# Weight sums moved from GpSimd to VectorE, and low parts of weights made by accumulating DMAs, in the pooling layer of a two-layer encoder trunk

## The chip, the cores and the metric

One core of a Trainium2 chip runs the whole program. The metric is the device time of one execution in microseconds (us). TensorE is called PE in the profile, VectorE DVE, ScalarE ACT, GpSimd POOL and SyncE SP; SP issues the plain loads.

## The reference

A sequence of 512 tokens of width 1024 passes two residual layers. The even layer (mLSTM heads and stick-breaking attention heads) is not touched by the change. The odd layer is:

```python
def odd_layer(x, pre_g, post_g, w_in, pool_w, pool_scale, w_out):
    h = rmsnorm(x, pre_g)
    u = h @ w_in                                  # 512x1024 @ 1024x4096
    p, z = u[..., :C_WIDTH], u[..., C_WIDTH:]     # 2048 columns each
    pooled = multiscale_pool(p.reshape(Bn, S, C_GROUPS, C_GROUP_DIM))   # windows 2, 4, 8, 16
    mixed = jnp.einsum('bsgc,gce->bsge', pooled, pool_w)                # 4 maps of 512x512
    mixed = mixed.reshape(Bn, S, C_WIDTH) * pool_scale
    y = (mixed * jax.nn.silu(z)) @ w_out                                # 512x2048 @ 2048x1024
    return x + rmsnorm(y, post_g)
```

`multiscale_pool` is the mean over a trailing window of each channel, one window for each group of 512 channels, minus the token itself. Everything is float32.

## The kernel before, in words

**Precision.** TensorE multiplies float32r, a rounded float32. Each operand x is kept as a high part, x rounded to float32r, and a low part, x minus the high part. A product is three matmuls (`mm3`, lines 95 to 97): high by high, high by low, low by high. `split` makes both parts: ACT copies with rounding into the high tile (line 71), then DVE subtracts it from x into the low tile (line 72). `halves` does that for weights, into the tiles `wh` and `wl`, of which four slots each go round in the order in which the program asks for them. A new weight block can be split only when TensorE has made the last use of the block four places earlier.

**Loads.** `load` brings 1024 KB of raw weights into one of two `w32` tiles, issued by SP (line 83).

**The odd layer** goes over four groups g = 0 to 3, with windows 2, 4, 8 and 16. Each group has two blocks p (columns to be pooled) and two blocks z (gates), named pg0, pg1, zg0, zg1, each 1024 by 256 weights against 512 tokens. Group 0's p comes from plain projections; the other 14 blocks go through `strassen2`, a seven-product scheme. It cuts a block of raw weights into a11, a12, a21, a22 (each 128 x 512 in a tile), and builds four sums on GpSimd (lines 695 to 698): s1 = a21 + a22, s2 = s1 + a11, s3 = a11 + a21, s4 = a12 + s2. Then it splits four weight tiles:

- a: the raw left half, a11 and a21 (128 x 1024), for the first two products,
- b: the sums s2 and s1 (128 x 1024),
- c: the sums s3 and s4 (128 x 1024),
- d: a22 (128 x 512), for the last product.

Each product is 12 matmuls of 256 columns. Products go into the banks psa, psb and pse, and DVE and ACT combine them (lines 715 to 732; the `pt` tiles hold partial results). The right-hand operands are blocks of the layer's input `hTh`/`hTl` and four combinations of them (d3, d1, n2, t4), which DVE forms once in `hidden_sums`.

**Pooling** of a group's four chunks of 128 channels: DVE adds shifted copies (line 762) and finishes with line 769; POOL divides the first few columns (lines 767, 768) and clears edges with memsets; `split` makes `pph` and `ppl`. The group's 512 x 512 map `pw` is split in two halves and multiplied with them in 48 matmuls of 512 columns into `mx`.

**Order.** The program is written in tiles, and a scheduler lays out each engine's instructions in one fixed order at build time. Each engine then works strictly in that order, waiting on semaphores. So a change of one operation reorders whole engines in the layer.

Of the kernel before, what the change touches and what calls it, by code (L numbers as in the profile page):

```python
# [5 lines left out]
F32 = mybir.dt.float32  # L6
F32R = mybir.dt.float32r
AF = mybir.ActivationFunctionType
ALU = mybir.AluOpType
# [4 lines left out]
P = 128  # L14
S = 512
# [21 lines left out]
def body(nc, tc, x, pre_g, post_g, w_in, conv, b_i, b_f, hn_g, w_out, w_in_c, pool_w,  # L37
         pool_scale, w_out_c, out):
    V, A, G, T = nc.vector, nc.scalar, nc.gpsimd, nc.tensor
# [4 lines left out]
    with base as base, psum as psum, dram as dram:  # L44
# [4 lines left out]
        def pj(name): return bank("pj", 2, name)  # L49
# [20 lines left out]
        def split(src, hi, lo):  # L70
            A.activation(hi, src, AF.Copy)  # L71
            V.tensor_tensor(lo, src, hi.bitcast(F32), op=ALU.subtract)  # L72

        def whl(name):
            return (base.tile([P, WIDE], F32R, tag="wh", bufs=4, name=f"wh_{name}"),
                    base.tile([P, WIDE], F32R, tag="wl", bufs=4, name=f"wl_{name}"))
# [9 lines left out]
        def halves(w, name, into=None):  # L86

            a, n = w.shape[1], w.shape[2]
            wh, wl = (t[:, :a * n].rearrange("p (a n) -> p a n", a=a) for t in (into or whl(name)))
            split(w, wh, wl)  # L90
            return wh, wl
# [110 lines left out]
        with tc.tile_pool(name="att", bufs=1) as at:  # L202
# [386 lines left out]
            for h in range(HA):  # L589
# [7 lines left out]
                for s in range(NB):  # L597
                    t = bc[:, ROW[s]:ROW[s] + P]
# [28 lines left out]
        with tc.tile_pool(name="odd", bufs=1) as od:  # L627
# [6 lines left out]
            def big(name, dtype=F32): return od.tile([P, D], dtype, tag="big", bufs=8, name=name)  # L634

            def ytiles(n):
                return (od.tile([P, S], F32R, tag="phi", bufs=5, name=f"yh_{n}"),
                        od.tile([P, S], F32R, tag="plo", bufs=5, name=f"yl_{n}"))

            ready = y_split(1, EVEN2[0], ytiles("first"), "e")  # L640
            xn = od.tile([P, NB, D], F32, name="xn")
# [28 lines left out]
            def ws(name): return od.tile([P, 8, P], F32, tag="ws", bufs=3, name=name)  # L670

            def hidden_sums():
                raw = {}
                b11, b21, b12, b22 = quarter(0, 0), quarter(1, 0), quarter(0, 1), quarter(1, 1)
                for n in ("d3", "d1", "n2", "t4"):
# [9 lines left out]
                        V.scalar_tensor_tensor(raw[n], raw["n2"], -1.0, b21, op0=ALU.mult, op1=ALU.subtract)  # L685
                    split(raw[n], *hs[n])

            def strassen2(src, name, dsts, silu=False):

                w = load(lambda t: [(nc.sync, t, src)], 8, 256, name)  # L690
                a11, a12, a21, a22 = (w[:, 4 * k:4 * k + 4, m * P:m * P + P]
                                      for m in range(2) for k in range(2))
                sums = [ws(f"ws{i}_{name}") for i in range(2)]
                s1, s2, s3, s4 = sums[0][:, 4:], sums[0][:, :4], sums[1][:, :4], sums[1][:, 4:]
                G.tensor_tensor(s1, a21, a22, op=ALU.add)  # L695
                G.tensor_tensor(s2, s1, a11, op=ALU.add)
                G.tensor_tensor(s3, a11, a21, op=ALU.add)
                G.tensor_tensor(s4, a12, s2, op=ALU.add)
                first = halves(w[:, :, :P], f"{name}_a")
                second = halves(sums[0], f"{name}_b")  # L700
                third = halves(sums[1], f"{name}_c")
                fourth = halves(a22, f"{name}_d")

                def product(ps, wt, k0, b, start, stop):
                    (wh, wl), (bh, bl) = wt, hs[b]
                    for k in range(4):
                        mm3(ps, (wh[:, k0 + k], wl[:, k0 + k]), (bh[:, k], bl[:, k]),
                            start and k == 0, stop and k == 3, skip_group_check=True)

                def part(i): return od.tile([P, 256], F32, tag="part", bufs=4, name=f"pt{i}_{name}")  # L710

                pa, pb, pe = (f(f"ps{n}_{name}")[:, :256] for f, n in ((pj, "a"), (xa, "b"), (xb, "e")))
                t1, t2, t5 = part(1), part(2), part(5)
                product(pa, first, 0, "11", True, True)
                A.activation(t1, pa, AF.Copy)
                product(pb, first, 4, "21", True, True)
                V.tensor_tensor(dsts[0][:, :256], pb, t1, op=ALU.add)
                product(pa, second, 0, "n2", False, True)
                A.activation(t2, pa, AF.Copy)
                product(pe, second, 4, "d1", True, True)  # L720
                A.activation(t5, pe, AF.Copy)
                product(pa, third, 0, "d3", False, True)
                V.scalar_tensor_tensor(dsts[1][:, 256:], pa, -1.0, t5, op0=ALU.mult, op1=ALU.subtract)
                product(pe, third, 4, "22", False, True)
                V.tensor_tensor(dsts[0][:, 256:], pe, t2, op=ALU.add)
                product(pa, fourth, 0, "t4", False, True)
                if silu:
                    act(dsts[0], dsts[0], AF.Silu)
                    act(dsts[1][:, 256:], dsts[1][:, 256:], AF.Silu)
                    act(dsts[1][:, :256], pa, AF.Silu, scale=-1.0)  # L730
                else:
                    A.activation(dsts[1][:, :256], pa, AF.Copy, scale=-1.0)

            for g, w in enumerate(WINDOWS):
                pooled = []
                cur4 = []
                for j in range(4):
                    c = 4 * g + j
                    cur = od.tile([P, 16 + S], F32, tag="win", bufs=6, name=f"p_{c}")
                    G.memset(cur[:, :16], 0.0)  # L740
                    cur4.append(cur)
                wsrc = [w_in_c[0, :, 512 * g + 256 * i:512 * g + 256 * i + 256] for i in range(2)]
                if g == 0:
                    wj = [t() for i in range(2) for t in col_load(wsrc[i], f"p{g}{i}")]
                    for j, n0 in ((j, n0) for n0 in (0, 256) for j in range(4)):
                        ps = pj(f"ps_p{4 * g + j}_{n0}")
                        col_proj(wj[j], ps, n0, n0 + 256)
                        A.activation(cur4[j][:, 16 + n0:16 + n0 + 256], ps[:, n0:n0 + 256], AF.Copy)
                    hidden_sums()
                else:  # L750
                    for i in range(2):
                        strassen2(wsrc[i], f"p{g}{i}", [t[:, 16:] for t in cur4[2 * i:2 * i + 2]])
                for j in range(4):
                    c = 4 * g + j
                    cur = cur4[j]
                    p32 = cur[:, 16:]
                    sh = 1
                    while sh < w:
                        nx = od.tile([P, 16 + S], F32, tag="win", bufs=6, name=f"p_{c}_{sh}")
                        if 2 * sh < w:  # L760
                            G.memset(nx[:, :16], 0.0)
                        V.tensor_tensor(nx[:, 16:], cur[:, 16:], cur[:, 16 - sh:16 + S - sh],  # L762
                                        op=ALU.add)
                        cur, sh = nx, 2 * sh
                    sm = cur[:, 16:]
                    e = w - 1
                    G.tensor_tensor(sm[:, :e], sm[:, :e], invc[:, :e], op=ALU.mult)
                    G.tensor_tensor(sm[:, :e], sm[:, :e], p32[:, :e], op=ALU.subtract)
                    V.scalar_tensor_tensor(sm[:, e:], sm[:, e:], 1.0 / w, p32[:, e:], op0=ALU.mult,
                                           op1=ALU.subtract)  # L770
                    ph = od.tile([P, S], F32R, tag="phi", bufs=5, name=f"pph{c}")
                    pl = od.tile([P, S], F32R, tag="plo", bufs=5, name=f"ppl{c}")
                    split(sm, ph, pl)
                    pooled.append((ph, pl))
                sz = []
                for i in range(2):
                    pair = [od.tile([P, S], F32, tag="sz", bufs=4, name=f"sz{4 * g + 2 * i + j}")
                            for j in range(2)]
                    strassen2(w_in_c[0, :, 2048 + 512 * g + 256 * i:2304 + 512 * g + 256 * i],
                              f"z{g}{i}", pair, True)  # L780
                    sz.extend(pair)
                w4 = load(lambda t: [(nc.sync, t, pool_w[0, g])], 4, 512, f"pw{g}")
                pw = [halves(w4[:, 2 * i:2 * i + 2], f"pw{g}{i}") for i in range(2)]
                for e in range(4):
                    c = 4 * g + e
                    ps = ac(f"mx{c}")
                    for k in range(4):
                        wh, wl = pw[k // 2]
                        mm3(ps, (wh[:, k % 2, e * P:e * P + P], wl[:, k % 2, e * P:e * P + P]),
                            pooled[k], k == 0, k == 3)  # L790
                    V.scalar_tensor_tensor(y32[:, c], ps, psc(c), sz[e], op0=ALU.mult, op1=ALU.mult)
# [44 lines left out]
```

## Time and profile before

| | us |
|---|---|
| median of 3 runs | 935.57 (935.47 to 936.04) |
| profiled execution | 938.04 |
| its span in the trace | 936.3 |
| odd layer's groups, in the span | about 605 to 845 |
| output map behind them | about 845 to 929 |

The profile counts the busy time of each engine in the span. In its timeline, idle time ahead of an instruction stands in square brackets with the instruction that ended it. The granted TensorE clock is given as a share of full speed for a stretch of time. Names in the trace leave out group numbers: `wl_z_a` is the low part of a of any z block.

### The profile page before, as it was taken

The numbers are of one execution on the slowest core, as the hardware profiler recorded it, in microseconds if no ns is written. First come the engines' busy times: TensorE is split into PE (matmuls) and PEld (weight loads), VectorE is DVE, ScalarE is ACT, GpSimd is POOL, SyncE is SP. The second block draws the span as 40 slices with busy tenths as digits, with TensorE's granted clock in tenths as the row PEclk, the third lists the DMA queues.
The fourth block names the chain that finished last, engine by engine and source line by source line (L and its number), as shares of the span: only waits on it lengthen the run. The fifth ranks groups of instructions, "written<-read, shape, count | busy, mean of one in ns | idle before, by whom it ended". The sixth has DMA issues, their size and how long they took to land. (4 is left out here: it accounts for less than half of the span.)

```text
span 936.3 us, 12756 instructions
## 1 busy us (share of the span) xinstructions
PE 903.9 (97%) x4957; PEld 783.1 (84%) x4957; DVE 603.9 (65%) x863; ACT 503.3 (54%) x850; POOL 170.4 (18%) x277
## 2 busy tenths in 40 slices
PE   8999999999999999999999999988989999889997
PEld 6788889888988898898888878888979988868885
DVE  5435555658876673854855556677695887957452
ACT  6436666665776554555467455654434544535331
POOL 2001111101102001010010000065565456510000
PEclk8999999999999999999999999998989999989998
DMA  8232221212222233223312645503122241346331
GB/s 293 89 93 66 71 90 46 90 48 88 80 97 90 85 93 127 91 91 124 96 45 90 225 174 196 169 1 130 51 91 90 91 136 46 114 134 223 109 117 46
DMA packets 67133, 98.97 MB, mean 106 GB/s; under 512 B 2848, under 2 KB 54136, under 8 KB 67072
## 3 DMA queue, kind: packets, MB, share of 16 engines
q1 hardware_dynamic: 65888, 98.08, 32.1%
q8 instruction: 39, 0.64, 0.3%
q10 hardware_dynamic: 1184, 0.08, 0.1%
q14 instruction: 22, 0.18, 0.1%
HBM read 96.02 MB, written 2.13 MB: 105 GB/s over the span
## 5 line engine op out<-in xcount | busy, mean ns | idle before, releaser
L97 PE MATMUL ps_qa<-hTh,wl_qa 128*128 128x512 f32 x128 | 50.3, 393 | 0.0
L95 PE MATMUL ps_qa<-hTh,wh_qa 128*128 128x512 f32 x128 | 50.2, 393 | 0.0
L96 PE MATMUL ps_qa<-hTl,wh_qa 128*128 128x512 f32 x128 | 50.2, 392 | 0.0
L72 DVE TENSOR_TENSOR wl_wo_e<-w_wo_e,wh_wo_e 128x1024 fp32r<-128x1024 f32 x28 | 34.3, 1233 | 23.5 <-ACT wh_wo_e L71 23.3
L71 ACT ACTIVATE wh_wo_e<-w_wo_e 128x1024 fp32r<-128x1024 f32 x28 | 29.4, 1057 | 29.0 <-DMA w_wo_e<-in_w_out_ab 13.6
L540 PE MATMUL op<-wh_wo_e,yl_e 128*128 128x512 f32 x120 | 39.1, 396 | 0.0
L540 PE MATMUL op<-wl_wo_e,yh_e 128*128 128x512 f32 x120 | 39.1, 396 | 0.0
L762 DVE TENSOR_TENSOR p<-p 128x512 f32<-128x512 f32 x40 | 37.9, 955 | 0.1
L540 PE MATMUL op<-wh_wo_e,yh_e 128*128 128x512 f32 x120 | 37.8, 395 | 0.0
L384 POOL TENSOR_TENSOR w<-w,w 128x384 f32<-128x384 f32 (+2 forms) x12 | 10.4, 869 | 144.8 <-DVE pl L72 135.9
L67 ACT ACT_TABLE_LOAD x28 | 35.9, 1283 | 1.3 <-PEq L821 0.8
L97 PE MATMUL psv_va<-wh_va,hTl 128*128 128x256 f32 x128 | 36.1, 282 | 0.0
L95 PE MATMUL psv_va<-wh_va,hTh 128*128 128x256 f32 x128 | 36.1, 282 | 0.0
L96 PE MATMUL psv_va<-wl_va,hTh 128*128 128x256 f32 x128 | 36.1, 282 | 0.0
L695 POOL TENSOR_TENSOR ws_z<-w_z 128x512 f32<-128x512 f32 x8 | 17.8, 2229 | 98.6 <-DVE d1l L72 69.0
L320 DVE SCALAR_TENSOR_TENSOR cv<-u,vecs,cv 128x511 f32<-128x511 f32 (+2 forms) x48 | 35.4, 748 | 0.4
L447 POOL TENSOR_SCALAR_AFFINE_SELECT a<-a 128x128 f32<-128x128 f32 x32 | 12.1, 387 | 126.9 <-DVE a L445 111.3
L72 DVE TENSOR_TENSOR wl_wo_o<-w_wo_o,wh_wo_o 128x1024 fp32r<-128x1024 f32 x20 | 24.3, 1224 | 12.0 <-ACT wh_wo_o L71 12.0
L72 DVE TENSOR_TENSOR wl_qa<-w_qa,wh_qa 128x1024 fp32r<-128x1024 f32 x16 | 19.6, 1222 | 18.4 <-ACT wh_qa L71 18.4
L540 PE MATMUL oq<-wl_wo_o,yh_o 128*128 128x512 f32 x96 | 31.3, 405 | 0.0
L540 PE MATMUL oq<-wh_wo_o,yh_o 128*128 128x512 f32 x96 | 31.3, 404 | 0.0
L71 ACT ACTIVATE wh_wo_o<-w_wo_o 128x1024 fp32r<-128x1024 f32 x20 | 20.9, 1053 | 19.2 <-PE oq L540 8.1
(430 smaller groups left out, 3210.1 us busy)
## 6 DMA issues: line engine op xcount, KB each, us to landing
w_wo_e<-in_w_out_ab SPq DMA_DIRECT2D x14, 1024.0 KB, 4.8
w_wo_o<-in_w_out_c SPq DMA_DIRECT2D x12, 1024.0 KB, 5.0
w_qa<-in_w_in_ab SPq DMA_DIRECT2D x8, 1024.0 KB, 5.0
w_p<-in_w_in_c SPq DMA_DIRECT2D x8, 1024.0 KB, 5.4
w_z<-in_w_in_c SPq DMA_DIRECT2D x8, 1024.0 KB, 5.3
w_qb<-in_w_in_ab SPq DMA_DIRECT2D x4, 1024.0 KB
w_kb<-in_w_in_ab SPq DMA_DIRECT2D x4, 1024.0 KB, 5.0
w_zb<-in_w_in_ab SPq DMA_DIRECT2D x4, 1024.0 KB, 5.0
```

Of the source, the lines that this page charges most:

```text
L67: link(A.preload_act_table_set(TABLE[func]))
L71: A.activation(hi, src, AF.Copy)
L72: V.tensor_tensor(lo, src, hi.bitcast(F32), op=ALU.subtract)
L95: T.matmul(dst, lhsT=ah, rhs=bh, start=first, stop=False, **kw)
L96: T.matmul(dst, lhsT=ah, rhs=bl, start=False, stop=False, **kw)
L97: T.matmul(dst, lhsT=al, rhs=bh, start=False, stop=last, **kw)
L320: V.scalar_tensor_tensor(acc[:, j:], u[:, :S - j], cw(3 - j, c), acc[:, j:], op0=ALU.mult, op1=ALU.add)
L384: G.tensor_tensor(total[:, t0:], total[:, t0:], w[:, t0:], op=ALU.add)
L447: G.affine_select(a[:, t0:t0 + P], a[:, t0:t0 + P], pattern=[[1, P]], base=-1, channel_multiplier=-1, compare_op=ALU.is_ge, fill=0.0)
L540: T.matmul(ps[a][n], lhsT=l[:, ta], rhs=r[:, 0, n * 512:n * 512 + 512], start=(first and l is yh and r is wh), stop=(last and l is yl))
L695: G.tensor_tensor(s1, a21, a22, op=ALU.add)
L762: V.tensor_tensor(nx[:, 16:], cur[:, 16:], cur[:, 16 - sh:16 + S - sh], op=ALU.add)
```

## The change

The four sums go from GpSimd to VectorE. For the raw weights, a and d, and for both halves of each pool map, a new function makes the low part without VectorE: ACT writes the rounded weights negated into the low tile, GpSimd issues DMAs that add the raw weights from memory onto it, and ACT writes the high tile as before. What lands is raw minus rounded, the same low part. A DMA covers 128 x 4 x 128 numbers (256 KB, in rows of 512 B) for a strassen block, two for a and one for d; and 128 x 2 x 512 (512 KB, in rows of 2 KB) for half a pool map. That is 14 x 3 + 4 x 2 = 50 DMAs. `fourth` (d) is asked for ahead of `third` (c), so the slots rotate in the order a, b, d, c.

To find room, the tiles `phi`, `plo` go from five to four and `part` from four to three, and the space for descriptors of GpSimd's DMAs grows from 1024 to 4096 bytes.

```diff
-                return (od.tile([P, S], F32R, tag="phi", bufs=5, name=f"yh_{n}"),
-                        od.tile([P, S], F32R, tag="plo", bufs=5, name=f"yl_{n}"))
+                return (od.tile([P, S], F32R, tag="phi", bufs=4, name=f"yh_{n}"),
+                        od.tile([P, S], F32R, tag="plo", bufs=4, name=f"yl_{n}"))
...
+            def halves_dma(w, src, name):
+                a, n = w.shape[1], w.shape[2]
+                wh, wl = (t[:, :a * n].rearrange("p (a n) -> p a n", a=a) for t in whl(name))
+                A.activation(wl, w, AF.Copy, scale=-1.0)
+                for i in range(0, a, min(a, 4)):
+                    G.dma_start(wl[:, i:i + min(a, 4)], src[:, i:i + min(a, 4)], accum_op=ALU.add)
+                A.activation(wh, w, AF.Copy)
+                return wh, wl
...
+                rows = src.rearrange("(a p) n -> p a n", p=P)
-                G.tensor_tensor(s1, a21, a22, op=ALU.add)
-                G.tensor_tensor(s2, s1, a11, op=ALU.add)
-                G.tensor_tensor(s3, a11, a21, op=ALU.add)
-                G.tensor_tensor(s4, a12, s2, op=ALU.add)
-                first = halves(w[:, :, :P], f"{name}_a")
+                first = halves_dma(w[:, :, :P], rows[:, :, :P], f"{name}_a")
+                V.tensor_tensor(s1, a21, a22, op=ALU.add)
+                V.tensor_tensor(s2, s1, a11, op=ALU.add)
                 second = halves(sums[0], f"{name}_b")
+                fourth = halves_dma(a22, rows[:, 4:, P:], f"{name}_d")
+                V.tensor_tensor(s3, a11, a21, op=ALU.add)
+                V.tensor_tensor(s4, a12, s2, op=ALU.add)
                 third = halves(sums[1], f"{name}_c")
-                fourth = halves(a22, f"{name}_d")
...
-                def part(i): return od.tile([P, 256], F32, tag="part", bufs=4, name=f"pt{i}_{name}")
+                def part(i): return od.tile([P, 256], F32, tag="part", bufs=3, name=f"pt{i}_{name}")
...
-                pw = [halves(w4[:, 2 * i:2 * i + 2], f"pw{g}{i}") for i in range(2)]
+                rows = pool_w[0, g].rearrange("(a p) n -> p a n", p=P)
+                pw = [halves_dma(w4[:, 2 * i:2 * i + 2], rows[:, 2 * i:2 * i + 2], f"pw{g}{i}")
+                      for i in range(2)]
...
-                    dynamic_dma_scratch_size=1024)
+                    dynamic_dma_scratch_size=4096)
```

The orders of the engines change at many places. Three matter for what follows. The rows give line, operation, written tile, read tiles and shape; here tile names do carry block and part (ws0 holds s2 and s1, ws1 holds s3 and s4), with a running number behind.

First, DVE at the start of the first strassen block, z00, where the operations on t4 end and b's low part is due. Before:

```order
L72 TENSOR_TENSOR n2l_5725<-raw_n2_5723,n2h_5724 128x1024
L762 TENSOR_TENSOR p_1_1_5744<-p_1_5477 128x512
L769 SCALAR_TENSOR_TENSOR p_0_1_5735<-p_0_1_5735,p_0_5475 128x511
L72 TENSOR_TENSOR t4l_5731<-raw_t4_5729,t4h_5730 128x1024
L72 TENSOR_TENSOR wl_z00_b_5786<-ws0_z00_5775,wh_z00_b_5785 128x1024
```

The same place after:

```order
L72 TENSOR_TENSOR t4l_5731<-raw_t4_5729,t4h_5730 128x1024
L709 TENSOR_TENSOR ws0_z00_5775<-ws0_z00_5775,w32_z00_5773 128x512
L712 TENSOR_TENSOR ws1_z00_5776<-w32_z00_5773 128x512
L781 SCALAR_TENSOR_TENSOR p_1_1_5744<-p_1_1_5744,p_1_5477 128x511
L774 TENSOR_TENSOR p_2_1_5753<-p_2_5479 128x512
L72 TENSOR_TENSOR ppl0_5741<-p_0_1_5735,pph0_5740 128x512
L708 TENSOR_TENSOR ws0_z01_5904<-w32_z01_5902 128x512
L713 TENSOR_TENSOR ws1_z00_5776<-w32_z00_5773,ws0_z00_5775 128x512
L729 TENSOR_TENSOR sz0_5771<-psb_z00_5801,pt1_z00_5803 128x256
L72 TENSOR_TENSOR wl_z00_b_5786<-ws0_z00_5775,wh_z00_b_5785 128x1024
```

Eight operations, four of them sums, now stand between t4l and wl_z00_b.

Second, ACT where block p10 hands over to p11 (weights a of p11 take the slot of a of p10). Before:

```order
L71 ACTIVATE wh_p10_c_6112<-ws1_p10_6099 128x1024
L71 ACTIVATE wh_p10_d_6116<-w32_p10_6096 128x512
L71 ACTIVATE wh_p11_a_6225<-w32_p11_6217 128x1024
L719 ACTIVATE pt2_p10_6124<-psa_p10_6120 128x256
L71 ACTIVATE wh_p11_b_6229<-ws0_p11_6219 128x1024
```

And after:

```order
L696 ACTIVATE wh_p10_d_6120<-w32_p10_6104 128x512
L693 ACTIVATE wl_p10_d_6121<-w32_p10_6104 128x512
L71 ACTIVATE wh_p10_c_6127<-ws1_p10_6107 128x1024
L696 ACTIVATE wh_p11_a_6232<-w32_p11_6228 128x1024
L693 ACTIVATE wl_p11_a_6233<-w32_p11_6228 128x1024
L71 ACTIVATE wh_p11_b_6240<-ws0_p11_6230 128x1024
```

The negative (L693) stands behind the rounding of the same tile, and the rounding of c of p10 has come directly ahead of both. On TensorE, the 40 matmuls of 256 columns between the last use of a of p10 and the first use of wl_p11_a are b of p10 on psa (12), the high parts of a of p11 (4) and c of p10 on psa and pse (24), and then:

```order
L95 MATMUL pse_p10_6133<-hTh_63,wh_p10_c_6127 128x256
L96 MATMUL pse_p10_6133<-hTl_64,wh_p10_c_6127 128x256
L97 MATMUL pse_p10_6133<-hTh_63,wl_p10_c_6128 128x256
L97 MATMUL psa_p11_6255<-hTh_63,wl_p11_a_6233 128x256
L95 MATMUL psa_p11_6255<-hTh_63,wh_p11_a_6232 128x256
```

Before, the matmuls with c on pse came behind a of p11, not ahead of it.

Third, POOL in group 2, around block z21. Before:

```order
L695 TENSOR_TENSOR ws0_z21_7141<-w32_z21_7139 128x512
L697 TENSOR_TENSOR ws1_z21_7142<-w32_z21_7139 128x512
L696 TENSOR_TENSOR ws0_z21_7141<-ws0_z21_7141,w32_z21_7139 128x512
L761 MEMSET p_10_1_6982 128x16
L767 TENSOR_TENSOR p_9_4_6973<-p_9_4_6973,invc_101 128x7
```

And after, L779 and L780 being the division and subtraction on the first columns:

```order
L695 DMA wl_z20_d_7059<-in_w_in_c 128x4x128
L773 MEMSET p_10_1_7010 128x16
L779 TENSOR_TENSOR p_9_4_7001<-p_9_4_7001,invc_101 128x7
L773 MEMSET p_10_2_7013 128x16
L780 TENSOR_TENSOR p_9_4_7001<-p_9_4_7001,p_9_6726 128x7
L695 DMA wl_z21_a_7175<-in_w_in_c 128x4x128 x2
```

The sums are gone, and the two DMAs of a of z21 wait in the queue behind the edge columns of chunk 9.

More of the change, by code (lines that the diff above doesn't have):

```diff
@@ L770, in body @@
                                            op1=ALU.subtract)
-                    ph = od.tile([P, S], F32R, tag="phi", bufs=5, name=f"pph{c}")
-                    pl = od.tile([P, S], F32R, tag="plo", bufs=5, name=f"ppl{c}")
+                    ph = od.tile([P, S], F32R, tag="phi", bufs=4, name=f"pph{c}")
+                    pl = od.tile([P, S], F32R, tag="plo", bufs=4, name=f"ppl{c}")
                     split(sm, ph, pl)
```

## The prediction

> **What bounds the kernel now.** The page first: TensorE is busy for nearly the whole span, so only its idle time and its clock are to be won. Then the windows of 20 us over the odd layer (us, then busy us and count of each engine, then granted clock and DMA), then what TensorE waited for there (total us, times, longest).
>
> ```profile
> PE 903.9 (97%) x4957; PEld 783.1 (84%) x4957; DVE 603.9 (65%) x863; ACT 503.3 (54%) x850; POOL 170.4 (18%) x277
> ...
> 620.00:640.00 20.00, 14.79 (x94) 13.79 (x92) 16.39 (x15) 8.36 (x14) 19.84 (x16) 0.83 0.03 7
> 640.00:660.00 20.00, 19.55 (x128) 18.48 (x129) 13.07 (x19) 9.56 (x16) 8.52 (x11) 0.91 0.45 152
> ...
> 680.00:700.00 20.00, 15.63 (x117) 15.23 (x116) 20.00 (x24) 8.53 (x14) 11.88 (x16) 0.89 0.34 107
> 700.00:720.00 20.00, 20.00 (x136) 18.85 (x136) 12.16 (x16) 9.55 (x17) 9.91 (x12) 0.94 0.34 106
> ...
> 820.00:840.00 20.00, 16.58 (x72) 13.38 (x71) 11.03 (x15) 8.03 (x12) 3.50 (x5) 0.83 0.45 153
> ```
>
> ```profile
> PE psa_z L97 <- DVE wl_z_a L72: 8.1, 4, 2.8
> PE mx L95 <- ACT pph L71: 3.3, 1, 3.3
> PE psb_z L95 <- DVE p L717: 3.3, 3, 1.6
> PE pse_z L95 <- ACT wh_z_b L71: 2.4, 1, 2.4
> PE psb_z L95 <- DVE sz L717: 1.4, 2, 0.8
> PE psa_z L97 <- DVE wl_z_c L72: 0.4, 1, 0.4
> ```
>
> With four smaller waits these make 20.0 us between 600 and 840. The clock below 1.00 costs 20 x (0.17 + 0.09 + 0.11 + 0.06 + 0.17) = 12.0 us more. It falls after the four stalls of 2.4 us and over, none of the shorter ones, so about 3.0 us each. **32.0 us** are lost in all, and no more can come back, since the matmuls stay the same.
>
> Why DVE is late shows in its timeline from 687 on (start, us), with POOL's instruction between:
>
> ```profile
> 687.40 0.68 DVE L769 SCALAR_TENSOR_TENSOR p<-p,p 128x509 f32<-128x509 f32 x1
> ...
> 688.33 1.99 DVE L72 TENSOR_TENSOR wl_z_c<-ws_z,wh_z_c 128x1024 fp32r<-128x1024 f32 x1
> ...
> 690.58 1.44 DVE L762 TENSOR_TENSOR p<-p 128x512 f32<-128x512 f32 x1
> 691.94 1.78 DVE L72 TENSOR_TENSOR wl_z_d<-w_z,wh_z_d 128x512 fp32r<-128x512 f32 x1
> 693.64 1.75 DVE L72 TENSOR_TENSOR ppl<-p,pph 128x512 fp32r<-128x512 f32 x1
> 695.32 1.21 DVE L72 TENSOR_TENSOR wl_z_a<-w_z,wh_z_a 128x1024 fp32r<-128x1024 f32 x1
> ...
> 691.43 1.74 POOL L696 TENSOR_TENSOR ws_z<-ws_z,w_z 128x512 f32<-128x512 f32 x1
> ...
> 696.58 0.58 PE L97 MATMUL psa_z<-hTh,wl_z_a 128*128 128x256 f32 x1 [2.76 <-DVE wl_z_a L72]
> ```
>
> While POOL adds, a 512-wide DVE operation of 0.68 us takes up to 1.78 us; with POOL idle it is back to its length. TensorE waits 2.76 us for a subtraction that is last in this queue. The Trainium skill (SBUF — State Buffer, Who interferes with whom) says that a DVE operation with two SBUF inputs and a reading GpSimd operation exclude each other; these rows agree.
>
> **The change part by part.** First DVE, ACT and POOL, by groups (count, busy us, mean ns):
>
> ```profile
> L762 DVE TENSOR_TENSOR p<-p 128x512 f32<-128x512 f32 x40 | 37.9, 955 | 0.1
> L72 DVE TENSOR_TENSOR wl_z_c<-ws_z,wh_z_c 128x1024 fp32r<-128x1024 f32 x8 | 12.2, 1519 | 0.1
> L72 DVE TENSOR_TENSOR wl_pw<-w_pw,wh_pw 128x1024 fp32r<-128x1024 f32 x8 | 9.8, 1222 | 3.2 <-ACT wh_pw L71 3.2
> L72 DVE TENSOR_TENSOR wl_z_a<-w_z,wh_z_a 128x1024 fp32r<-128x1024 f32 x8 | 9.7, 1214 | 0.0
> L71 ACT ACTIVATE wh_z_a<-w_z 128x1024 fp32r<-128x1024 f32 x8 | 8.4, 1053 | 1.6 <-PE psa_p L96 1.6
> L71 ACT ACTIVATE wh_z_d<-w_z 128x512 fp32r<-128x512 f32 x8 | 5.0, 625 | 3.7 <-PE psb_z L96 3.7
> L761 POOL MEMSET p<- 128x16 f32 x24 | 2.7, 110 | 14.3 <-DVE ppl L72 10.1 <-DVE p L762 3.4 <-DVE p L769 0.7
> L767 POOL TENSOR_TENSOR p<-p,invc 128x15 f32<-128x15 f32 x4 | 7.4, 1848 | 10.6 <-DVE p L762 10.6
> ```
>
> *DVE.* Removed: 14 subtractions of a (1.21 us), 14 of d (0.68), 8 of the pool map (1.22), 36 us. Added: 56 sums of 512 columns at 0.68, 38 us. The contention goes with POOL's sums: 40 x (955 - 680) ns is 11 us on L762 alone, and 8 x (1519 - 1220) ns 2.4 on wl_z_c. So DVE loses over 11 us, all of it in the windows where it is full, and the 13.2 us that TensorE waits for DVE should go (8.1 + 3.3 + 1.4 + 0.4), with the clock behind them. POOL keeps edge columns, memsets, and now 50 DMA issues.
>
> *ACT* gains 14 x (1.05 + 0.63) + 8 x 1.05 = 32 us over some 200; at 8 to 10 of 20 us busy it has the room, and I cost the load at nothing; its order I don't, below.
>
> *The new chain.* The low part of a was one subtraction behind ACT's rounding. Now, once TensorE frees the slot: ACT rounds, ACT writes the negative, POOL issues two DMAs, they land. From these rows, slot to negative is 0.2 + 1.05 + 1.05 = 2.3 us. No accumulate stands in the trace. Nearest rows (KB, median us from issue to landing):
>
> ```profile
> w_z<-in_w_in_c SPq DMA_DIRECT2D x8, 1024.0 KB, 5.3
> out<-xo SPq DMA_DIRECT2D x8, 256.0 KB, 2.3
> y<-in_x SPq DMA_DIRECT2D x2, 256.0 KB, 3.2
> g_post<-in_post_norm_g SPq DMA_DIRECT2D x2, 512.0 KB, 3.5
> ```
>
> Each half of a is 256 KB, so 2.3 is the lower end. An add must also read what is there; both halves together then move as much as a 1024 KB load, 5.3, the upper end. POOL's issue lies between 0.1 (a memset) and 1.85 (L767); I take 0.5. First half doubled: 3.5 + 0.5; both halves plain, the second needed ten matmuls later: 3.5 + 0.5 - 1.2; both doubled: 5.3 + 0.5 - 1.2 = 4.6. I take X = **4.0 us** from negative to usable, and keep 2.4 and 5.3 as ends. The slot-to-use latency is L = 2.3 + 4.0 = 6.3 us. The Trainium skill (DMA: Bandwidth & Descriptors, Anatomy of one DMA) fits 2.0 us plus bytes at 436 GB/s, an estimate of 2.6 us for 256 KB; by that the result would be rival one below. No run here shows it.
>
> What covers L is the matmuls between the last use of the old slot and the first use of the new low part. Their pace:
>
> ```profile
> 647.28 0.28 PE L95 MATMUL pse_z<-d1h,wh_z_b 128*128 128x256 f32 x1
> 647.40 0.28 PE L96 MATMUL pse_z<-d1l,wh_z_b 128*128 128x256 f32 x1
> ...
> 650.14 0.39 PE L95 MATMUL mx<-pph,wh_pw 128*128 128x512 f32 x1
> 650.37 0.40 PE L96 MATMUL mx<-ppl,wh_pw 128*128 128x512 f32 x1
> ```
>
> 0.12 us for 256 columns, 0.23 for 512. Counted over the new TensorE order, the cover of a is, in us: p10 6.55, p11 4.7, z10 6.1, z11 7.55, p20 5.4, p21 5.1, z20 6.1, z21 7.55, p30 2.6, p31 6.6, z30 5.4, z31 6.1. p11 is the pattern: 40 matmuls of 256. For p11, p21 and p31 ACT has a rounding of c first (the order above shows it), 0.75 late; and the wait for c itself gives p11 and p21 0.35 of cover. So TensorE waits 2.0 at p11, 0.95 at p20, 1.6 at p21, 3.7 at p30, 0.45 at p31, 0.85 at z30, and 0.15 at z10, z20 and z31: **10.0 us**, and p30's is long enough for a clock drop, 3.0. d (7 to 10 us of cover, 1.5 on ACT) and the pool map (8 to 9 us) I cost at nothing: the products of the other blocks hide them; if X passes 5.5 they show.
>
> *Kept or new waits.* c of p10, p20 and p30 now takes the slot that the pool map left last, 2.4 to 2.7 us of cover against 1.05 + 1.22 + 0.3 and queueing: 0.35 each, 1.0. In the first block, z00, TensorE waited for POOL:
>
> ```profile
> 617.44 7.41 POOL L695 TENSOR_TENSOR ws_z<-w_z 128x512 f32<-128x512 f32 x1 [68.98 <-DVE d1l L72]
> ...
> 622.49 1.22 DVE L72 TENSOR_TENSOR t4l<-raw_t,t4h 128x1024 fp32r<-128x1024 f32 x1
> 627.32 1.61 DVE L72 TENSOR_TENSOR wl_z_b<-ws_z,wh_z_b 128x1024 fp32r<-128x1024 f32 x1 [3.61 <-ACT wh_z_b L71]
> ...
> 627.34 0.46 PE L95 MATMUL pse_z<-d1h,wh_z_b 128*128 128x256 f32 x1 [2.41 <-ACT wh_z_b L71]
> ```
>
> That 7.41 us goes, but wl_z_b now stands behind eight operations after t4l. t4l starts 0.5 us earlier (one subtraction out, one sum in) and ends at 623.2, seven operations started 0.6 apart and one half as wide follow, and wl_z_b is done at 628.9, as before. TensorE came to wh_z_b at 624.9 and is at wl_z_b four matmuls later, 625.4: 3.4 of waiting and 3.0 of clock stay, and what follows it (0.4, 2.45) goes. At the end, mx waits 3.3 us behind ACT's table load; the new order sets that rounding ahead of the load: 1.0 left. Small waits before 616: 0.7. POOL's edge columns now stand ahead of the z DMAs in its queue: 2.0.
>
> *Other moves.* Four phi/plo tiles instead of five and three parts change the order in the even output map, where TensorE is at 20.00 of 20; they are hidden by its matmuls. If a tile were missing it would show as a wait on ACT's yh there. SP's loads wait for the last reader of w32, now the negative of d or s4 instead of the subtraction of d, no later. The DMAs add 14 x 768 + 8 x 512 KB, 15 MB, to engines at a share of 0.03 to 0.45.
>
> **Sum.** After: 6.4 + 0.7 + 1.0 + 10.0 + 3.0 + 1.0 + 2.0 = 24.1 us lost, against 32.0: 7.9 us gained. The profiled execution took 938.04 us (span 936.3), 2.5 over the median of 935.57; the gain is taken from the median: **927.7 us**.
>
> **Rivals.** One: the DMAs are hidden. X = 2.6: the waits for a shrink to 3.1 (p30 2.3, p11 0.6, p21 0.2), no clock drop, no queue term: 12.2 lost, **916 us**. For it: 2.3 and 3.2 us rows; against: none of them adds.
>
> Two, the other side: accumulating is slow. X = 5.3, a full 1024 KB row: L = 7.6, waits of 3.3, 2.9 and 5.0 at p11, p21 and p30, 22.8 in all, three clock drops, 42.9 lost: **946.5 us**. Between 4.0 and 5.3 each us of X costs 14.5, so it decides from X = 4.6 on. For it: both halves doubled give exactly 4.6; against: DMA share is low. The Trainium skill (Collectives: The Full Stack, The bandwidth ceiling) says that a reduce step's add needs two source reads and so gets half the rate of a copy; by that X is 4.6, on the edge, and any queueing puts the time on this side. No run here shows it yet.
>
> Three: DVE, now dense with two-input operations, holds up POOL's descriptor writing, as it held L695 for 7.41 us. At 3 us on each of six z blocks, +18 and three clock drops: **955 us**. Against: memsets, which read nothing, took 0.11 us in the same windows. The Trainium skill (SBUF — State Buffer, Who interferes with whom) holds that tensor_tensor leaves descriptor writing alone; by that this rival falls.
>
> **Numbers.** Forecast 0.47, rival one 0.14, two 0.29, three 0.07, and 0.03 for something in the order that I don't see. 0.2% (1.9 us) is about what a measurement tells from no change; X from 4.4 to 4.7 lands within it. Faster 0.53 (rival one and most of the forecast), same 0.10, slower 0.37. The range runs from rival one to just past rival two, 915 to 950; the forecast alone, X 3.4 to 4.5, is 920 to 935.
>
> **What would show it.** DVE's 512-wide operations at 0.68 throughout; no wait of TensorE on wl_z_a of DVE, but on the low parts of a from DMA, longest at p30; issue to landing near 3.5 us; wh_z_b at 625 and wl_z_b at 629. Wrong it is if landing takes over 4 us, if POOL's issues take over 1 us, or if waits on d or the pool map appear.

## The result and the profile after

The changed kernel takes 957.66 us (956.81 to 962.27) against 935.52 us (932.05 to 936.04) on the same chip: ratio 1.0255, 95% interval 1.0214 to 1.0296. It is 22 us slower, where 7.9 us less was forecast. The profiled execution took 962.27 us, 4.6 above the median, with a span of 960.5.

From the page after, the busy times and the two DMA queues (q1 the plain loads, q0 GpSimd's adds: packets, MB, share of 16 engines):

```profile
PE 912.2 (95%) x4957; PEld 787.4 (82%) x4957; DVE 578.6 (60%) x883; ACT 528.3 (55%) x886; POOL 134.7 (14%) x271
...
q1 hardware_dynamic: 65888, 98.08, 31.2%
q0 software_dynamic: 24352, 15.21, 12.0%
```

The 4957 matmuls are the same as before, so TensorE's line splits the loss. It is busy 8.3 us longer (912.2 against 903.9) and idle 15.9 us longer (960.5 - 912.2 = 48.3 against 936.3 - 903.9 = 32.4). Together that is the 24.2 us that the span has grown. The clock is little of the first part: over windows of 20 us of the whole span, what the granted clock lacks to 1.00 comes to 17.8 us before and 20.0 after. What makes up the other 6 us of busy time isn't known.

Windows of 20 us of after, as those shown of before:

```profile
640.00:660.00 20.00, 15.86 (x113) 14.48 (x112) 5.80 (x10) 11.58 (x18) 6.23 (x5) 1.00 0.93 188
...
700.00:720.00 20.00, 17.26 (x126) 15.93 (x124) 7.91 (x14) 13.36 (x21) 8.49 (x15) 1.00 0.92 182
720.00:740.00 20.00, 16.16 (x78) 13.99 (x78) 8.10 (x11) 4.59 (x7) 1.27 (x1) 0.83 0.40 69
```

VectorE is now busy for 6 to 8 of 20 us in these windows, and in the first two the DMA engines are nearly full instead: 0.92 from 700 to 720, where 0.34 stood. What TensorE waited for in the odd layer after, and what the DVE operation that had been slowed now takes:

```profile
PE mx L97 <- DMA wl_pw<-in_pool_w: 15.2, 8, 4.2
PE psa_z L97 <- DMA wl_z_a<-in_w_in_c: 8.1, 7, 1.9
PE psb_z L97 <- DMA wl_z_a<-in_w_in_c: 3.0, 5, 1.0
...
PE psa_p L97 <- DMA wl_p_a<-in_w_in_c: 2.4, 1, 2.4
PE psa_p L97 <- DMA wl_p_d<-in_w_in_c: 1.6, 1, 1.6
PE psa_z L97 <- DVE wl_z_b L72: 1.2, 1, 1.2
```

```profile
L774 DVE TENSOR_TENSOR p<-p 128x512 f32<-128x512 f32 x40 | 27.1, 687 | 1.0 <-POOL p L780 0.3
```

Of the waits for DVE 1.2 us is left; 30.3 us are waits for low parts that a DMA makes. How long one takes is in the groups of GpSimd (a DMA's row there is its issue: count, busy us, mean ns) and in the list of DMA issues of the odd layer (KB, median us from issue to landing):

```profile
L695 POOL DMA_DIRECT2D wl_z_a<-in_w_in_c x16 | 21.1, 1568 | 92.9 <-DVE d1l L72 69.1 <-ACT wl_z_a L693 9.3 <-ACT pt_p L731 7.7
...
L695 POOL DMA_DIRECT2D wl_pw<-in_pool_w x8 | 9.6, 1199 | 14.4 <-ACT wl_pw L693 8.6 <-ACT pt_z L731 3.8 <-PE psa_z L97 2.0
```

```profile
w_z<-in_w_in_c SPq DMA_DIRECT2D x7, 1024.0 KB, 6.3
w_p<-in_w_in_c SPq DMA_DIRECT2D x6, 1024.0 KB, 8.9
...
wl_z_a<-in_w_in_c POOLq DMA_DIRECT2D x16, 256.0 KB, 5.4
...
wl_pw<-in_pool_w POOLq DMA_DIRECT2D x8, 512.0 KB, 8.0
wl_p_a<-in_w_in_c POOLq DMA_DIRECT2D x12, 256.0 KB, 7.9
```

A pair of issues takes 2.6 us of GpSimd (21.1 us for 16, 1.3 each; the mean of 1568 ns is longer because the records of a pair overlap), the landing, counted from the start of the issue, 5.4 to 8.0, and the plain loads of p have slowed from 5.3 to 8.9. The longest stall shows the chain, from the timeline of after (ACT's negative, the issue, the matmul that waited):

```profile
711.28 1.05 ACT L693 ACTIVATE wl_pw<-w_pw 128x1024 fp32r<-128x1024 f32 x1
...
712.74 1.20 POOL L695 DMA_DIRECT2D wl_pw<-in_pool_w  x1 [1.98 <-PE psa_z L97]
...
723.59 0.80 PE L97 MATMUL mx<-pph,wl_pw 128*128 128x512 f32 x1 [4.17 <-DMA wl_pw<-in_pool_w]
```

From the negative's end at 712.33 to the first use 11.3 us pass. The first block tells what a landing takes with nothing else in flight: SP issues no load between 601 and 628. The windows of 4 us of after (columns as above):

```profile
616.00:620.00 4.00, 4.00 (x34) 4.00 (x35) 4.00 (x6) 3.63 (x6) 2.59 (x3) 1.00 0.06 7
620.00:624.00 4.00, 3.82 (x31) 3.45 (x29) 4.00 (x6) 0.38 (x1) 4.00 (x2) 1.00 1.02 123
```

The two halves of a, 0.52 MB, keep all 16 engines busy for 4.3 us (0.06 x 4 + 1.02 x 4). They landed 4.9 us (the first) and 6.4 us (the second) after their issues at 617.4 and 618.4, as the instructions on `wl_z_a` between 616 and 620 show:

```profile
DMA to landing us min/median/max: 4.9/5.7/6.4
```

### The profile page after: what moved, and what is told of

Read it like the earlier page. It is cut to its first block, busy times and chain, and to the rows that moved or that the text cites. A ratio compares the mean times of both kernels' runs of the same rounds, so it can differ in the third digit from the quotient of the medians.

```text
span 960.5 us, 12883 instructions
## 1 busy us (share of the span) xinstructions
PE 912.2 (95%) x4957; PEld 787.4 (82%) x4957; DVE 578.6 (60%) x883; ACT 528.3 (55%) x886; POOL 134.7 (14%) x271
## 3 DMA queue, kind: packets, MB, share of 16 engines
q1 hardware_dynamic: 65888, 98.08, 31.2%
q0 software_dynamic: 24352, 15.21, 12.0%
## 4 chain that ended last, share of the span: by engine, by line
PE 80%; DMA 9%; issue 4%; ACT 3%; POOL 2%; DVE 2%; SPq 0%; DVEq 0%; ACTq 0%; POOLq 0%
PE op L540 9%; PE oq L540 9%; DMA wl_z_a<-in_w_in_c 4%; DMA wl_pw<-in_pool_w 3%; PE ps_qa L97 3%; PE ps_qa L96 3%; PE ps_qa L95 3%; PE psv_va L97 2%; PE psv_va L95 2%; PE psv_va L96 2%; PE ps_zb L95 2%; PE ps_oa L97 2%; PE ps_oa L96 2%; PE ps_za L95 2%; PE ps_zb L97 2%
## 5 line engine op out<-in xcount | busy, mean ns | idle before, releaser
L97 PE MATMUL mx<-pph,wl_pw 128*128 128x512 f32 x64 | 27.8, 446 | 15.2 <-DMA wl_pw<-in_pool_w 15.2
L695 POOL DMA_DIRECT2D wl_z_a<-in_w_in_c x16 | 21.1, 1568 | 92.9 <-DVE d1l L72 69.1
L72 DVE TENSOR_TENSOR wl_qa<-w_qa,wh_qa 128x1024 fp32r<-128x1024 f32 x16 | 19.6, 1223 | 18.4 <-ACT wh_qa L71 18.4
L540 PE MATMUL oq<-wh_wo_o,yl_o 128*128 128x512 f32 x96 | 30.3, 396 | 0.0
```

The lines of the kernel that those rows point to most:

```text
L97: T.matmul(dst, lhsT=al, rhs=bh, start=False, stop=last, **kw)
L540: T.matmul(ps[a][n], lhsT=l[:, ta], rhs=r[:, 0, n * 512:n * 512 + 512], start=(first and l is yh and r is wh), stop=(last and l is yl))
L695: G.dma_start(wl[:, i:i + min(a, 4)], src[:, i:i + min(a, 4)], accum_op=ALU.add)
```

## The experiments

Every kernel ran beside the kernel before; its time is the median, and the ratio to before has its interval. The median of the kernel before lay between 934.9 and 935.9 us in every set of runs, so times of different sets are compared directly. "Control" is the changed kernel with all low parts back on VectorE.

**Which part of the change.** The sums alone, on the kernel before:

```diff
-                G.tensor_tensor(s1, a21, a22, op=ALU.add)    # s2, s3, s4 alike
+                V.tensor_tensor(s1, a21, a22, op=ALU.add)
```

> The kernel before with the four sums of a weight block on VectorE instead of GpSimd and nothing else: all low parts are VectorE subtractions, phi/plo tiles 5, parts 4. Theory A (the change loses its time in the accumulating DMAs: they are issued late and land late, and TensorE waits for the low parts; the sums are harmless): 925 to 937 us, since the slowed VectorE operations (0.68 us taking up to 1.78) go back to 0.68 and 38 us of sums come in; in the z blocks VectorE is at 17 to 20 of 20 us either way. Rival B (VectorE, with 38 us more, is what holds TensorE up in the changed kernel): 945 us or more, with TensorE waiting on VectorE for wl_z_b, wl_z_c and wl_p_c.

920.94 us, ratio 0.983 (0.980 to 0.987). The sums on VectorE are a gain of 14.7 us, more than theory A had (925 to 937 us); rival B is out.

The opposite, the DMAs without the sums:

```diff
-                V.tensor_tensor(s1, a21, a22, op=ALU.add)    # in the changed kernel; s2, s3, s4 alike
+                G.tensor_tensor(s1, a21, a22, op=ALU.add)
```

> The changed kernel with the four sums put back on GpSimd: only the DMAs of the change. Theory A: worse than the changed kernel's 957.7 us, 962 to 985 us, since the DMA issues of 1.2 to 1.3 us each now stand in one queue with 56 sums of 1.2 to 1.9 us, and the low parts of a come later still. Rival B (the sums on VectorE hurt): under 950 us.

979.35 us, 1.046 (1.043 to 1.049), as theory A said. The sums take 1.6 to 2.2 us each there, in the queue that issues the DMAs.

The changed kernel without any DMA:

```diff
-                first = halves_dma(w[:, :, :P], rows[:, :, :P], f"{name}_a")    # d and the pool map alike
+                first = halves(w[:, :, :P], f"{name}_a")
```

> The changed kernel with all low parts back to VectorE's subtraction: it keeps the sums on VectorE, the new order of the four sums and roundings, phi/plo 4, parts 3 and the larger descriptor scratch, but issues no accumulating DMA. Theory A (the DMAs' lateness is the whole loss): as the sums alone, 917 to 925 us. Rival D (the smaller pools and the new order carry part of the loss): 928 us or more, and that part has to be taken off what the DMAs are charged with.

918.74 us, 0.982 (0.981 to 0.984). Smaller pools and the new order cost nothing; all 38.9 us between this and 957.7 belong to making low parts by DMA: the DMAs, the slots that they hold, and ACT's negatives, which no run has by themselves. Its waits in the odd layer:

```profile
PE psa_z L95 <- ACT wh_z_b L71: 3.2, 1, 3.2
PE mx L95 <- ACT pph L71: 2.7, 1, 2.7
PE psa_z L97 <- DVE wl_z_b L72: 1.8, 1, 1.8
```

**Which of the DMAs.** Without the pool map's:

```diff
-                pw = [halves_dma(w4[:, 2 * i:2 * i + 2], rows[:, 2 * i:2 * i + 2], f"pw{g}{i}")
+                pw = [halves(w4[:, 2 * i:2 * i + 2], f"pw{g}{i}")
```

> The changed kernel with the pool map's low parts (wl_pw) back to VectorE's subtraction; a and d stay with the DMAs. Theory A (latency of each low part): the 15.2 us that TensorE waits for wl_pw go, and the clock behind its stalls of 4.2 and 3.4 us, some 3 us each: 934 to 941 us; the waits for the low part of a stay near 13.5 us (8.1 + 3.0 + 2.4). Rival C (the bytes: 15 MB of accumulating traffic slow the weight loads, and all is late for that): the pool map is 4 of 15 MB, so a quarter of the 22 us goes, 950 to 954 us.

938.73 us, 1.0035 (1.0017 to 1.0052): 18.9 us back. Its waits for the low part of a are 15.2 us.

With the pool map's alone:

```diff
-                pw = [halves(w4[:, 2 * i:2 * i + 2], f"pw{g}{i}")            # in the control
+                pw = [halves_dma(w4[:, 2 * i:2 * i + 2], rows[:, 2 * i:2 * i + 2], f"pw{g}{i}")
```

> The changed kernel with a and d back to VectorE's subtraction; sums on VectorE and only the pool map by accumulating DMAs. Theory A: TensorE waits for wl_pw as in the changed kernel, 12 to 17 us with two clock drops, and VectorE has 28 us more than there: 942 to 952 us, and the excess over a kernel with the sums alone is the same 16 to 22 us that the pool map's return takes from the changed kernel. Rival C (bytes): 4 of 15 MB give some 6 us over the kernel with the sums alone.

931.80 us, 0.996 (0.994 to 0.998): 13.1 over the control, less than the 16 to 22 expected, and below the 942 to 952, which had been reckoned from a slower time for the sums. The pool map alone puts its wait on TensorE:

```profile
PE mx L97 <- DMA wl_pw<-in_pool_w: 7.4, 5, 2.8
```

With d's alone:

```diff
-                fourth = halves(a22, f"{name}_d")            # in the control
+                fourth = halves_dma(a22, rows[:, 4:, P:], f"{name}_d")
```

> The control with d alone by accumulating DMA (14 DMAs of 256 KB); a, the pool map and the sums on VectorE. Theory A (a landing costs only what the matmuls ahead of its use do not cover; d has 7 to 10 us of cover against 1.3 of issue and 5 to 8 of landing): 918 to 923 us, at most 2 us of waits for wl_p_d and wl_z_d. Rival C (each of these DMAs costs its share: 14 of 50 DMAs, 3.7 of 15.2 MB, of the 39 us between the control and the changed kernel): 927 to 931 us.

918.82 us, 0.982 (0.980 to 0.984). No cost, and no wait for wl_z_d or wl_p_d in the trace, though they land 6.9 and 6.7 us after the issue. So a costs 938.73 - 918.82 = 19.9 us (on top of d), the pool map 13.1, d 0.1. They sum to 33.1; the remaining 5.8 of 38.9 come only with all together.

**What in a DMA.** The same DMAs writing instead of adding:

```diff
-                    G.dma_start(wl[:, i:i + min(a, 4)], src[:, i:i + min(a, 4)], accum_op=ALU.add)
+                    G.dma_start(wl[:, i:i + min(a, 4)], src[:, i:i + min(a, 4)])
```

> The changed kernel with the same DMAs at the same places from the same queue, but writing in place of adding (the low parts then are the raw weights, so the numbers computed differ; no instruction is added or removed). Theory A1 (the add makes the landing slow: 5.4 to 8.0 us for 256 and 512 KB against 2.3 to 3.5 for plain rows): landing 2.5 to 4.5 us, the waits for low parts (31 us) fall to under 14, 930 to 943 us. Theory A2 (descriptors written by GpSimd and small rows make it slow, the add is free): issue still 1.3 us, landing 5 us and more, 952 to 960 us.

933.85 us, 0.997 (0.995 to 0.999): 23.8 of the 38.9 us are the add. Issue (of the groups of GpSimd), queue (of the page) and landing (of the DMA issues in the odd layer):

```profile
L695 POOL DMA_DIRECT2D wl_z_a<-in_w_in_c x16 | 12.4, 774 | 81.6 <-DVE d1l L72 69.1 <-ACT wl_z_a L693 4.7 <-ACT pt_p L731 4.7
```

```profile
q0 software_dynamic: 24352, 15.21, 8.0%
```

```profile
wl_z_a<-in_w_in_c POOLq DMA_DIRECT2D x16, 256.0 KB, 3.6
wl_pw<-in_pool_w POOLq DMA_DIRECT2D x8, 512.0 KB, 5.3
```

The issue falls too, from 1.3 to 0.77 us each (12.4 us for 16); A2 had it at 1.3. A1's landing of 2.5 to 4.5 holds for z's a, not for p's a (4.9), d (5.7 and 5.9) or the pool map. The plain loads of p are back at 5.4 us, from 8.9.

Then the wait itself: the matmuls read the rounded weights where they read the low part, so none waits for a landing.

```diff
                 A.activation(wh, w, AF.Copy)
-                return wh, wl
+                return wh, wh
```

> The changed kernel with every accumulating DMA, negative and slot in place, but the matmuls read the rounded weights wh where they read the low part wl (so the numbers differ): nothing waits on TensorE for a landing, while GpSimd's queue, ScalarE's work and the traffic stay. Theory A (TensorE's waits for the landings are the loss): 919 to 928 us, next to the control's 918.7. Rival C (the traffic and the busy queues delay everything else: loads, memsets, edge columns): 940 us or more, with waits on other things.

952.48 us, 1.018 (1.012 to 1.023): only 5.2 us back, and not sharply known, since its four runs spread from 945.2 to 956.6. Theory A in its first form, that TensorE's own waits are the loss, fell here, and the time is in rival C's range. The loads are still late (8.2 us for p, 7.9 for z), and VectorE waits 30.6 and 17.4 us for them. And the slot of a low part is still taken until the DMA lands, and whoever wants it next waits, as the waits of ACT, of DVE and of PE show:

```profile
ACT wl_z_a L693 <- DMA wl_p_d<-in_w_in_c: 12.9, 3, 5.9
```

```profile
DVE wl_z_c L72 <- DMA wl_z_a<-in_w_in_c: 6.2, 1, 6.2
```

```profile
PE psa_z L97 <- DVE wl_z_c L72: 5.0, 1, 5.0
```

**Traffic or slots.** A first attempt ran the control with the same adds into a tile that nobody reads, 4 KB a partition.

```diff
+            def shadow(dst, wh, src):                 # dst: parts of one tile "dum"; called behind halves
...
+                G.tensor_copy(dst[:, 0, :2], wh[:, 0, :2].bitcast(F32))
+                for i in range(0, n, min(n, 4)):
+                    G.dma_start(dst[:, i:i + min(n, 4)], src[:, i:i + min(n, 4)], accum_op=ALU.add)
...
-                    dynamic_dma_scratch_size=4096)
+                    dynamic_dma_scratch_size=2560)
```

> The control (no low part by DMA, all by VectorE) with the same accumulating DMAs, as many, as large and at the same places in GpSimd's queue, released by ScalarE's rounding, but into a tile that nobody reads (descriptor scratch 2560 instead of 4096, for room). Theory A (latency: TensorE stands because it waits for these landings): no one waits, so 918 to 927 us, the plain loads slower by 1 to 3 us but still hidden. Rival C (the traffic itself delays the weight loads, so everything is late): 936 us or more, with waits behind w_p and w_z. Edge columns and memsets of GpSimd behind the issues may add up to 4 us in either.

990.77 us, 1.060 (1.057 to 1.062). That is within rival C's "936 us or more", but for another reason, so it tells nothing of the traffic: the copy that releases a DMA waits for the DMA before it on the same tile, and everything in GpSimd's queue with it.

```profile
POOL dum L705 <- DMA dum<-in_w_in_c: 87.2, 25, 6.5
POOL dum L705 <- DMA dum<-in_pool_w: 32.2, 6, 7.0
```

The second uses four rows of y32 in turn, which are free until the last pool map:

```diff
+                    dst = spare[:, 512 * u:512 * (u + e)].rearrange("p (a n) -> p a n", n=m).bitcast(F32R)
+                    G.tensor_copy(dst[:, 0, :2], wh[:, i, :2].bitcast(F32))
+                    G.dma_start(dst, src[:, i:i + min(n, 4)], accum_op=ALU.add)
```

> The control (all low parts by VectorE) with the same accumulating DMAs into four rows of y32 that are not in use yet, each released by a two-column copy from the rounded weights on GpSimd; only the last pool map's two are left out (the rows are written there), 14.2 of 15.2 MB. No low-part slot and no matmul waits for a landing. Theory A (the loss is in slots held from the negative to the landing, and in the waits for it): 919 to 928 us. Rival C (the traffic and the GpSimd queue delay loads, memsets and edge columns): 935 us or more, with VectorE's sums waiting for w_p.

938.86 us, 1.0034 (1.0008 to 1.006). Rival C has a share: with no low-part slot and no matmul behind the adds, they cost 20 us. (Only GpSimd's copies wait for a landing, 8 us in all, since the four rows come round again.) VectorE stands for loads that are late (its waits, then the DMA issues in the odd layer):

```profile
DVE ws_p L726 <- DMA w_p<-in_w_in_c: 11.3, 4, 4.8
DVE ws_z L726 <- DMA w_z<-in_w_in_c: 9.7, 4, 5.3
```

```profile
w_z<-in_w_in_c SPq DMA_DIRECT2D x7, 1024.0 KB, 6.8
w_p<-in_w_in_c SPq DMA_DIRECT2D x6, 1024.0 KB, 8.2
```

The same without the DMAs:

```diff
-                    G.dma_start(dst, src[:, i:i + min(n, 4)], accum_op=ALU.add)
```

> The run with the adds into unread rows, without its DMAs: only the 48 two-column copies on GpSimd remain over the control. Theory G (GpSimd's queue: memsets and edge columns stand behind copies that wait for ScalarE): 930 us or more, and the unread adds themselves cost less than 9. Theory C (the DMAs, by traffic and issue): 918 to 923 us.

922.08 us, 0.987 (0.985 to 0.989). The copies are 3.3 of the 20 us, the DMAs 16.8.

The same with plain writes in place of adds:

```diff
-                    G.dma_start(dst, src[:, i:i + min(n, 4)], accum_op=ALU.add)
+                    G.dma_start(dst, src[:, i:i + min(n, 4)])
```

> The run with the adds into unread rows, with the DMAs writing instead of adding: same bytes from memory, same copies and places. Theory C1 (the add's time on the DMA engines and on GpSimd's issue, 1.3 against 0.75 us, delays the loads): 921 to 929 us, w_p back to 5.5 us. Theory C2 (any software DMA traffic of this size costs that): 935 to 940 us.

928.62 us, 0.994 (0.992 to 0.996): 6.5 for the DMAs, 10.2 more for the add, as C1 said. But w_p does not come back to 5.5 (the DMA issues, then GpSimd's group):

```profile
w_p<-in_w_in_c SPq DMA_DIRECT2D x6, 1024.0 KB, 7.8
```

```profile
L714 POOL DMA_DIRECT2D y<-in_w_in_c x42 | 31.8, 759 | 8.2 <-POOL y L713 7.9 <-POOL p L771 0.3
```

So in these two runs slow loads come with either kind, while in the changed kernel plain writes left them at 5.4; what sets this isn't known. Whether the add's 10.2 us act through the engines' time or through GpSimd's longer issues isn't separated.

**Slots and descriptor space.** The changed kernel with a fifth low-part slot, and 2048 bytes of descriptor space to make room:

```diff
-                    base.tile([P, WIDE], F32R, tag="wl", bufs=4, name=f"wl_{name}"))
+                    base.tile([P, WIDE], F32R, tag="wl", bufs=5, name=f"wl_{name}"))
...
-                    dynamic_dma_scratch_size=4096)
+                    dynamic_dma_scratch_size=2048)
```

> The changed kernel with five slots for low parts instead of four (scratch 2048 for room), so that ScalarE's negative and the DMAs of a block can start when the slot of one block earlier is free. Theory A (the chain from free slot to landed low part, about 2.3 + 1.3 to 2.6 + 5.4 to 8 us, is longer than the 4.7 to 9 us of matmuls that cover it): the cover grows by a block, 2.4 to 9 us, most of the 31 us of waits for low parts go, 928 to 944 us. Rival C (traffic): the same traffic, 950 us or more.

1002.61 us, 1.073 (1.069 to 1.076): far above theory A and, though within rival C's "950 us or more", above the changed kernel with the same traffic. To see why, only the space, with four slots:

```diff
-                    dynamic_dma_scratch_size=4096)
+                    dynamic_dma_scratch_size=2048)
```

> The changed kernel with the descriptor scratch at 2048 instead of 4096, nothing else. Theory E (the run with five low-part slots was slow because 2048 holds one 256 KB DMA of 512 rows at a time: the second issue waited 3.6 to 6.2 us for the first to land): 985 to 1010 us, with GpSimd idle ahead of its issues for no semaphore. Rival F (the fifth slot itself did harm): 955 to 962 us, as the changed kernel.

1027.46 us, 1.098 (1.096 to 1.100): beyond the range, on theory E's side. The smaller space costs 70 us. The second issue of a pair waits until the first has landed (8.5 us after its start at 661.56), without a semaphore, as GpSimd's waits and timeline of that run show:

```profile
POOL wl_p_a L695 <- issue: 40.0, 7, 7.5
```

```profile
661.56 1.29 POOL L695 DMA_DIRECT2D wl_p_a<-in_w_in_c  x1 [2.34 <-ACT sz L68]
670.33 1.28 POOL L695 DMA_DIRECT2D wl_p_a<-in_w_in_c  x1 [7.48 <-issue]
```

Between these two runs only the fifth slot differs, and it gives back 24.9 us. So the number of slots counts when a slot is held long; what a fifth would give at 4096 wasn't run, for want of room.

The other direction:

```diff
-                    dynamic_dma_scratch_size=4096)
+                    dynamic_dma_scratch_size=6144)
```

> The changed kernel with 6144 of descriptor scratch instead of 4096, nothing else. Rival E (the scratch still binds: DMAs wait for room although no wait is shown): 930 to 950 us, with issue to landing shorter. Theory A (two 256 KB DMAs fit in 4096 and no issue waited for room): 954 to 961 us, as the changed kernel.

959.59 us, 1.026 (1.023 to 1.029), as the changed kernel. At 4096 the space no longer binds.

**A better version.** The control with its free room as a fourth ws tile (descriptor space 1024 again):

```diff
-            def ws(name): return od.tile([P, 8, P], F32, tag="ws", bufs=3, name=name)
+            def ws(name): return od.tile([P, 8, P], F32, tag="ws", bufs=4, name=name)
```

> The control (sums on VectorE, no DMA) with the descriptor scratch back at 1024 and the room spent on a fourth ws tile, so that the first block's sums need not wait for the raw hidden sums' tiles. The control waits 3.2 us for wh_z_b and 1.8 for wl_z_b in the first block, and loses 3.4 us to the clock behind them. If the ws tiles are what holds the sums: 910 to 916 us. If VectorE's queue is: 917 to 921 us.

918.72 us, 0.982 (0.980 to 0.984), no better than the control: the wait for wh_z_b falls from 3.2 to 1.1 us, but that for wl_z_b grows from 1.8 to 3.2, so VectorE's queue holds the first block, not the tiles. No version found is faster than the control, at 17 us less than before.

## Why the prediction was wrong, point by point

**The sums and VectorE: right, the gain too high.** VectorE's operations came back to 0.69 us, and TensorE's waits for it fell to 1.2. Without the DMA terms (10.0 + 3.0 + 2.0) the sum left 9.1 of 32.0 us lost, a gain of 22.9; the control gained 17.2. The first block loses 5.0 us and 3.4 to the clock where 6.4 stood, and the pool map's wait on pph (2.7) kept more than the 1.0 taken.

**"X = 4.0 us": too small, the step that failed first.** The rows nearest to it were plain, and the quiet add shows what they lacked: 4.9 us alone for the first half, 6.4 for the second, before any collision. Later blocks share the engines and land after 5.4 to 7.9; the issue is 1.3 us each, where 0.5 was taken; at the pool map X was 11.3 in the longest case. The rows that would show it wrong, landing over 4 us, issues over 1 us, waits on the pool map and d, all appeared.

**The waits for a: near in sum, not in place.** TensorE waited 13.5 us for them after (8.1 + 3.0 + 2.4), where the sum had 10.0. But 11.1 of these stand at z blocks, where it had 1.3, and the 2.4 are one wait at p21; p30, forecast as the longest with 3.7, shows none. In p10, p20 and p30 the stalls for the pool map stand ahead; why p11 and p31 have none isn't worked out. So the nearness is in part luck. The clock did not follow its rule either (a drop after stalls of 2.4 us and over, none after shorter ones): behind the stall of 3.38 us that ended at 659.62 the windows of 4 us to 672 show 1.00, and behind one of 1.56 us at 810.18 the window from 812 shows 0.61.

**"d and the pool map I cost at nothing": right for d, wrong for the pool map.** d costs 0.1 us by itself; the pool map costs 13.1 alone and 18.9 as the last one added, the largest miss of the sum. Its cover, put at 8 to 9 us, was below its chain. a was put at 15.0 us and costs 19.9.

**The DMAs' bytes at nothing, and loads "no later": wrong.** The sum named 15 MB on engines at a share of 0.03 to 0.45 and charged no time. Unread, the adds cost 16.8 us. The engines' share counts their time, not bytes: q0 took 12.0% of 960.5 us for 15.21 MB, 7.6 us of all 16 engines for each MB; q1 31.2% for 98.08 MB, 3.1 us.

**The rest of the 38.9 us** is put down to what the landing holds up: 38.9 - 16.8 leaves 22.1 us for TensorE's waits and the four slots that stay taken until the landing. That taking away the reading alone brings only 5.2 fits one wait taking the other's place, but no run removes both with the DMAs in place. ACT's negatives are in the 22.1 too; that they cost little is argued, not shown: d's 14, with their DMAs, cost 0.1. The split treats the parts as independent, and they are so only roughly.

**The rivals.** Two (accumulating is slow) was the right mechanism, from X = 4.6 on; 946.5 us is too low, since it too charged nothing for the pool map and the traffic. The Trainium skill (Collectives: The Full Stack, The bandwidth ceiling) says that a reduce step, whose add reads two sources, gets half the rate of a copy. Here the same bytes took 115.3 us of the engines with the add (12.0% of 960.5) and 74.5 without (8.0% of 930.9), a factor of 1.55; for this the measurement decides. One (hidden) fell. Three (VectorE holds up descriptor writing) did not show: the eight issues of the pool map took 1182 to 1223 ns wherever they fell, and with plain writes 0.72 us in the mean beside the same VectorE work. That its 955 us lies nearest to the result is coincidence.

So 24 of the 30 us between 927.7 and 957.7 are the DMAs, 38.9 instead of 15.0, and 5.7 the sums.

## What to carry to other kernels

Moving work from a compute engine to a DMA changed its price here from throughput to latency: compare issue plus landing, with the add, to the matmuls between the slot's release and the first use, and charge the slot for all that time. Only the part with long cover (d) was free, and then it bought nothing, since VectorE was no longer the bound. Charge DMAs by their engines' time, not their bytes, and test each part of a bundled change alone: here one part was worth 17 us and the other cost 38.9.

## What was not expected of the hardware

- An accumulating DMA took GpSimd 1.3 us to issue for 256 KB, and 0.75 to 0.78 us without the add; memsets of 16 columns took 466 ns in the mean in the changed kernel, 114 in the one with plain writes, 110 in the control.
- The descriptor space binds without a trace of a semaphore: at 2048 bytes the second 256 KB DMA is issued only when the first has landed, at 4096 two go out back to back; 70 us between them, and nothing from 4096 to 6144.
- A quiet 256 KB DMA from GpSimd landed after 3.5 and 3.9 us without the add (the two halves of a in the first block, the second issued before the first had landed), 4.9 and 6.4 with it:

```profile
DMA to landing us min/median/max: 3.5/3.7/3.9
```

These times hold the issue itself, 0.97 and 0.76 us without the add, so 2.5 and 3.1 are left behind it. The Trainium skill (DMA: Bandwidth & Descriptors, Anatomy of one DMA) fits 2.0 us plus bytes at 436 GB/s, an estimate of 2.6. The plain writes come near it once the issue is taken off; the adds (1.45 and 1.78 us of issue, so 3.4 and 4.6) do not.
